# Two gate projections tied behind the layer's last conv transposes, and these transposes spread over four PSUM banks

## Chip, cores and metric

The kernel runs on one NeuronCore of a Trainium2 chip. The metric is the device time of one execution in microseconds; the time before is the median of three runs, 2527.41 us.

## What is computed

A trunk of two layers on 512 tokens of width 1024, all in float32. Each layer applies a half-step SwiGLU FFN, gated parallel token mixers, and a second half-step FFN. The change is in the mixer, where three branches A, B and C are computed from one input projection, gated and summed; B is the convolution module:

```
h = _rmsnorm(x, mix_norm_pre[l])
proj = h @ w_in[l]
...
ob = _conformer_conv(conv_in, conv_w[l], conv_b[l], conv_norm_g[l], conv_norm_b[l])
...
gates = jax.nn.sigmoid(gate_pre + b_gate[l]).reshape(b, s, N_BRANCH, D_MODEL)
merged = gates[:, :, 0] * ya + gates[:, :, 1] * yb + gates[:, :, 2] * yc
x = x + _rmsnorm(merged @ w_out[l], mix_norm_post[l])
```

`_conformer_conv` is a GLU, a causal depthwise convolution of width 31 over 512 channels, a LayerNorm over the channels, and a silu; `yb` is its result times `w_proj_b`, and `gates[:, :, 1]` is the sigmoid of 1024 columns of `proj`.

## The kernel before

A float32 product runs as three matmuls: each operand is split into a rounded part (`hi`, ScalarE, line 120) and the rest (`lo`, VectorE, line 121), and lines 138, 139 and 140 multiply lo by hi, hi by hi and hi by lo. Weights come by the sync queue in pieces of 1 MB (`raw`, two buffers) and are split into `hi` and `lo` tiles, four of each. A gate projection (`gate`, through `proj_t`) is eight such triples, 24 matmuls of 512 columns, into a bank of tag `pm`; ScalarE then takes the sigmoid into `gt` (line 751).

PSUM has eight banks, by tag: three `pm`, two `ps`, two `pt`, one `po`. `ps` and `pt` serve the attention before this place and the FFNs.

The order of the instructions on each engine is set by a scheduler from the order of the program text and from what each instruction waits for. `tc.issue_after(x)` adds an edge: what is issued within comes behind `x` on its engine. The convolution is done on VectorE as 31 multiply-adds for each of four chunks of 128 channels (`taps`, line 498, tiles `y`, list `ys`). They are queued, and each split releases some of them behind itself. What is left when branches A and C are done is tied behind the last multiply of a gate (`flush`, line 758).

Then, for the convolution branch, in this order of the text:

- lines 778 to 789: for each of four groups of 128 tokens, four transposes (line 781, one per channel chunk) bring `ys` to tokens in one bank; VectorE takes statistics (lines 784, 785), ScalarE the square root (line 214, in `rstd`), VectorE the reciprocal (line 215) and the normalization into `yn` (line 788);
- lines 790 to 794: for each channel chunk, four transposes (line 793) bring `yn` back to channels in a `pt` bank, and ScalarE applies the silu (line 794);
- lines 795 to 797: the results are split into `ob` pairs (lines 464, 465);
- lines 798 to 809: for four pairs of output chunks, two gates and two products with `ob` (`branch`, lines 138 to 140, then line 758), the sum with the other branches on GpSimd (line 806), and the split of the sum (lines 808, 809).

ScalarE loads a table (ACT_TABLE_LOAD) when it goes from one of square root, sigmoid and silu to another.

Of the kernel before, what the change touches and what calls it, by code (L numbers as in the profile page):

```python
# [18 lines left out]
P = 128  # L19
# [30 lines left out]
def kernel(ctx: ExitStack, tc: tile.TileContext, a, out):  # L50
    nc = tc.nc
    V, S, G, PE, SY = nc.vector, nc.scalar, nc.gpsimd, nc.tensor, nc.sync

    def bc(t):
        return t.bitcast(F32)
# [7 lines left out]
    def bank(tag, shape=(P, T)):  # L63
        return psum.tile(list(shape), F32, tag=tag, name=tag, bufs=BANKS[tag])
# [24 lines left out]
    ident = per.tile([P, P], F32, name="ident")  # L89
# [24 lines left out]
    def split(raw, into=None):  # L114
        if into is None:
            hi = wp.tile(list(raw.shape), F32R, tag="hi", name="hi", bufs=HLB)
            lo = wp.tile(list(raw.shape), F32R, tag="lo", name="lo", bufs=HLB)
        else:
            hi, lo = into
        S.activation(hi, raw, AF.Copy)  # L120
        last = V.tensor_sub(lo, raw, bc(hi))  # L121
        for _ in range(min(pace[0], len(tapq))):
            tapq.pop(0)(last)
        return hi, lo
# [6 lines left out]
    def col_chunks(src, c0, c1, step=256):  # L131
        for c in range(c0, c1, step):
            raw = load(src[:, c:c + step], KD, step)
            for s in range(0, step, P):
                yield c + s, split(raw[:, :, s:s + P])
# [6 lines left out]
    def proj_group(chunks, hh, hl):  # L142
        ps = [bank("pm") for _ in chunks]
        for p_, (wh, wl) in zip(ps, chunks):
            for k in range(KD):
                mm3(p_, wh[:, k, :], wl[:, k, :], hh[:, k, :], hl[:, k, :], k == 0, k == KD - 1)
        return ps
# [63 lines left out]
    def rstd(ms, tag, bias=None, scale=1.0):  # L211
        n = ms.shape[1]
        r = sp.tile([P, n], F32, tag="rstd" + tag, name="rstd", bufs=4 if n == 1 else 1)
        S.activation(r, ms, AF.Sqrt, bias=eps[:, 0:1] if bias is None else bias, scale=scale)
        V.reciprocal(r, r)
        return r
# [217 lines left out]
    def mixer(l):  # L434
# [5 lines left out]
        def proj_t(chunk):  # L440
            return proj_group([chunk], hh, hl)[0]

        mrg = tc.tile_pool(name="mrg", bufs=1, side="right", reuse_waits="tile")
        with tc.tile_pool(name="mix", bufs=1, reuse_waits="tile") as mp:
# [13 lines left out]
            def ztile(n, name):  # L458
                return mp.tile([P, n], F32, tag="zr", name=name, bufs=ZRB)
# [12 lines left out]
            with tc.tile_pool(name="att", bufs=1, reuse_waits="tile") as ap:  # L472
                ys = []
# [189 lines left out]
                for h in range(4):  # L663
                    for i in range(NT):
                        V.tensor_scalar_mul(oc[h][:, i, :], oc[h][:, i, :], orr[:, h * 4 + i:h * 4 + i + 1])
                    pt = bank("pt")
# [9 lines left out]
                for b in range(NT):  # L676
# [3 lines left out]
                    for h in range(4):  # L680
                        r = slice(64 * (h % 2), 64 * (h % 2) + 64)
                        ps = bank("ps", (P, n))
# [12 lines left out]
                for r4 in range(4):  # L695
                    po = bank("po", (P, 4, HD))
                    cols = slice(r4 * P, (r4 + 1) * P)
                    for h in range(4):
                        r = slice(64 * (h % 2), 64 * (h % 2) + 64)
                        ps = bank("ps", (P, 256))  # L700
# [26 lines left out]
                for f in range(2):  # L727
                    pt = bank("pt", (P, 4, P))
# [9 lines left out]
            def mpair(d):  # L738
                return tuple(gp.tile([P, T], F32R, tag=f"m{u}{d}", name="m" + u) for u in "hl")

            gch = [col_chunks(wi, GT0 + b * D, GT0 + (b + 1) * D) for b in range(3)]

            def gate(b, d, first):
                ps = proj_t(next(gch[b])[1])
                gt = ztile(T, "gt")
                bias = late[:, b * 8 + d:b * 8 + d + 1]
                if first:
                    S.activation(gt, ps, AF.Copy)
                    S.activation(gt, gt, AF.Sigmoid, bias=bias)
                else:  # L750
                    S.activation(gt, ps, AF.Sigmoid, bias=bias)
                return gt

            def branch(gt, wh, wl, k0, hls):
                ps = bank("pm")
                for k, (mh, ml) in enumerate(hls):
                    mm3(ps, wh[:, k0 + k, :], wl[:, k0 + k, :], mh, ml, k == 0, k == len(hls) - 1)
                return V.tensor_mul(gt, gt, ps)

            for dp in range(0, KD, 2):  # L760
                gts = [[gate(b, dp + j, dp == 0) for j in range(2)] for b in (2, 0)]
                wca = wp.tile([P, KD, 256], F32, tag="raw", name="wca", bufs=2)
                cols = slice(dp * P, (dp + 2) * P)
                SY.dma_start(wca[:, 0:4, :], a["w_proj_c"][l][:, cols].rearrange("(k p) n -> p k n", p=P))
                SY.dma_start(wca[:, 4:6, :], a["w_proj_a"][l][:, cols].rearrange("(k p) n -> p k n", p=P))
                for j in range(2):
                    wh, wl = split(wca[:, 0:6, j * P:(j + 1) * P])
                    branch(gts[0][j], wh, wl, 0, oc_hl)
                    flush = branch(gts[1][j], wh, wl, 4, oa_hl)
                    m_ = ring(F32, "m")  # L770
                    G.tensor_add(m_, gts[0][j], gts[1][j])
                    ms.append(m_)
# [3 lines left out]
            pace[0] = 0  # L776
            yn = []
            for t in range(NT):
                pn = bank("pt")
                for c in range(NCH):  # L780
                    PE.transpose(pn[:, c * P:(c + 1) * P], ys[c][:, t * P:(t + 1) * P], ident)
                bs = sp.tile([P, 6], F32, tag="bs", name="bs")
                mv = sp.tile([P, 2], F32, tag="mv", name="mv", bufs=4)
                V.bn_stats(bs, pn)
                V.bn_aggr(mv, bs)
                r = rstd(mv[:, 1:2], "ln")
                n_ = sp.tile([P, T], F32, tag="t2k", name="yn", bufs=5)
                V.tensor_scalar(n_, pn, mv[:, 0:1], r, op0=ALU.subtract, op1=ALU.mult)
                yn.append(n_)
            for c in range(NCH):  # L790
                pt = bank("pt")
                for t in range(NT):
                    PE.transpose(pt[:, t * P:(t + 1) * P], yn[t][:, c * P:(c + 1) * P], ident)
                S.activation(ys[c], pt, AF.Silu, bias=cbn[:, c:c + 1], scale=cg[:, c:c + 1])
# [1 line left out]
            for c in range(NCH):  # L796
                put(ob_hl[c], ys[c])
            for dp in range(0, KD, 2):
                gts = [gate(1, dp + j, False) for j in range(2)]
                wb = wp.tile([P, KD, 256], F32, tag="raw", name="wb", bufs=2)  # L800
                cols = slice(dp * P, (dp + 2) * P)
                SY.dma_start(wb[:, 0:4, :], a["w_proj_b"][l][:, cols].rearrange("(k p) n -> p k n", p=P))
                for j in range(2):
                    wh, wl = split(wb[:, 0:4, j * P:(j + 1) * P])
                    branch(gts[j], wh, wl, 0, ob_hl)
                    G.tensor_add(gts[j], gts[j], ms[dp + j])
                    mm.append(mpair(dp + j))
                    S.activation(mm[dp + j][0], gts[j], AF.Copy)
                    V.tensor_sub(mm[dp + j][1], gts[j], bc(mm[dp + j][0]))
# [27 lines left out]
    for l in range(L):  # L837
        ffn(a["ffn1_norm_pre"][l], a["ffn1_norm_post"][l], a["ffn1_w_gate"][l], a["ffn1_w_up"][l], a["ffn1_w_down"][l],
            (gain0[0], raws0) if l == 0 else None)
        mixer(l)  # L840
        ffn(a["ffn2_norm_pre"][l], a["ffn2_norm_post"][l], a["ffn2_w_gate"][l], a["ffn2_w_up"][l], a["ffn2_w_down"][l])
# [62 lines left out]
```

## Time and profile before

| | us |
|---|---|
| median of three runs | 2527.41 (2525.86 to 2529.16) |
| the profiled execution | 2526.2 |
| its span | 2524.4 |
| TensorE busy in the span | 2465.5 |
| VectorE busy | 1735.6 |
| ScalarE busy | 1174.8 |
| GpSimd busy | 246.9 |

The span goes from the first to the last instruction of the profiled execution; its own time is 1.8 us longer. Times in views are counted from the start of the span. PE is TensorE's matmuls, PEld its weight loads (which overlap the matmuls), DVE is VectorE, ACT ScalarE, SPq the issue of a transfer by the sync engine. A matmul is listed with its start and the time to its modelled end; the next starts before that end, so the pace is read from the starts. A row of the timeline ends with the idle time ahead of it on its engine and what ended it, in brackets, where there was some.

### The profile page before, as it was taken

How to read it: one execution, taken by the hardware profiler on the slowest of the kernel's cores; microseconds unless marked ns; L12 is line 12 of the kernel's file. 1: busy time of each engine (PE TensorE's matmuls, PEld its weight loads, DVE VectorE, ACT ScalarE, POOL GpSimd, SP SyncE). 2: the span in 40 equal slices, each digit the busy share in tenths (PEclk: the TensorE clock that was granted, in tenths of full speed). 3: DMA queues.
4: the chain of work that ended last, by engine and by line, in shares of the span. 5: the costliest groups of instructions: out<-in, count | busy, mean ns of one | idle time of the engine just before them, and what ended most of it. 6: DMA issues, size and time to landing. Idle time of an engine off the chain costs nothing.

```text
span 2524.4 us, 36883 instructions
## 1 busy us (share of the span) xinstructions
PE 2465.5 (98%) x14956; PEld 2190.3 (87%) x14956; DVE 1735.6 (69%) x2354; ACT 1174.8 (47%) x1953; POOL 246.9 (10%) x156
## 2 busy tenths in 40 slices
PE   8999999999999999999989999999899999999999
PEld 8999888778787889998889998887787878899987
DVE  8777554796577487775497774546965764877753
ACT  5545444633523354445454454446235244544552
POOL 0000012060011110000000000130600111100000
PEclk9999999999999999999999999999999999999999
DMA  4333335242132423333233332451421224233322
GB/s 160 105 108 114 105 123 169 73 129 81 43 96 76 162 72 108 110 101 109 76 106 112 101 108 101 136 163 54 133 89 39 92 75 159 76 101 101 110 100 75
DMA packets 211850, 261.92 MB, mean 104 GB/s; under 512 B 8160, under 2 KB 167264, under 8 KB 211424
## 3 DMA queue, kind: packets, MB, share of 16 engines
q1 hardware_dynamic: 204000, 249.06, 30.1%
q10 hardware_dynamic: 7680, 10.50, 1.6%
q8 instruction: 118, 1.93, 0.3%
q14 instruction: 52, 0.43, 0.1%
HBM read 237.47 MB, written 6.29 MB: 97 GB/s over the span
## 4 chain that ended last, share of the span: by engine, by line
PE 88%; DVE 7%; ACT 2%; issue 2%; DMA 1%; SPq 0%; DVEq 0%; ACTq 0%
PE pm L138 11%; PE pm L139 11%; PE pm L140 11%; PE ps L308 6%; PE ps L314 6%; PE ps L313 6%; PE pm L313 2%; PE pm L308 2%; PE pm L314 2%; DVE y L498 2%; PE ps L139 2%; PE ps L140 2%; PE ps L138 2%; DVE lo L121 2%; PE pt L140 2%; PE pt L138 2%
## 5 line engine op out<-in xcount | busy, mean ns | idle before, releaser
L121 DVE TENSOR_TENSOR lo<-raw,hi 128x1024 fp32r<-128x1024 f32 x354 | 458.5, 1296 | 380.3 <-ACT hi L120 380.3
L120 ACT ACTIVATE hi<-raw 128x1024 fp32r<-128x1024 f32 x354 | 373.7, 1057 | 324.0 <-PE ps L139 127.2
L138 PE MATMUL pm<-hb,lo 128*128 128x512 f32 (+1 forms) x848 | 325.0, 383 | 0.0
L139 PE MATMUL pm<-hb,hi 128*128 128x512 f32 (+1 forms) x848 | 324.2, 382 | 0.0
L140 PE MATMUL pm<-hb,hi 128*128 128x512 f32 (+1 forms) x848 | 323.7, 382 | 0.0
L308 PE MATMUL ps<-t,lo 128*128 128x256 f32 x960 | 272.2, 284 | 4.3 <-ACT pm L381 4.3
L314 PE MATMUL ps<-t,hi 128*128 128x256 f32 x960 | 271.7, 283 | 0.0
L313 PE MATMUL ps<-t,hi 128*128 128x256 f32 x960 | 271.6, 283 | 0.0
L121 DVE TENSOR_TENSOR lo<-s,hi 128x1024 fp32r<-128x1024 f32 x160 | 194.9, 1220 | 69.1 <-ACT hi L120 68.9
L498 DVE SCALAR_TENSOR_TENSOR y<-z,ppl,y 128x512 f32<-128x512 f32 x240 | 214.4, 894 | 4.1
L120 ACT ACTIVATE hi<-s 128x1024 fp32r<-128x1024 f32 x160 | 164.8, 1052 | 88.4 <-DVE s L379 87.2
L308 PEld LDWEIGHTS ps<-t,lo 128*128 128x128 f32 x960 | 184.2, 192 | 5.3 <-ACT pm L381 5.3
L138 PEld LDWEIGHTS pm<-hb,lo 128*128 128x128 f32 x848 | 159.6, 188 | 31.9 <-issue 1.8
L139 PEld LDWEIGHTS pm<-hb,hi 128*128 128x128 f32 x848 | 159.5, 188 | 29.9 <-issue 0.7
L140 PEld LDWEIGHTS pm<-hb,hi 128*128 128x128 f32 x848 | 159.5, 188 | 29.9 <-issue 0.8
L314 PEld LDWEIGHTS ps<-t,hi 128*128 128x128 f32 x960 | 184.3, 192 | 0.0
L313 PEld LDWEIGHTS ps<-t,hi 128*128 128x128 f32 x960 | 184.3, 192 | 0.0
L240 POOL TENSOR_TENSOR h<-x,gain 128x512 f32<-128x512 f32 x40 | 54.0, 1370 | 1128.8 <-DVE x L299 1087.8
L120 ACT ACTIVATE ih<-inner 128x512 fp32r<-128x512 f32 x176 | 106.0, 622 | 82.6 <-PE ps L140 49.1
L121 DVE TENSOR_TENSOR il<-inner,ih 128x512 fp32r<-128x512 f32 x176 | 118.0, 687 | 38.3 <-ACT ih L120 38.3
L308 PE MATMUL pm<-hb,lo 128*128 128x256 f32 x480 | 135.8, 283 | 0.0
L313 PE MATMUL pm<-hb,hi 128*128 128x256 f32 x480 | 135.8, 283 | 0.0
(331 smaller groups left out, 6153.9 us busy)
## 6 DMA issues: line engine op xcount, KB each, us to landing
raw<-in_w_in_dram SPq DMA_DIRECT2D x62, 1024.0 KB, 5.4
raw<-in_ffn_w_gate_dram SPq DMA_DIRECT2D x43, 1024.0 KB, 5.0
raw<-in_ffn_w_up_dram SPq DMA_DIRECT2D x43, 1024.0 KB, 5.0
raw<-in_ffn_w_down_dram SPq DMA_DIRECT2D x40, 1024.0 KB, 4.9
sw<-raw ACTq DMA_DIRECT2D x160, 64.0 KB, 2.0
raw<-in_w_out_dram SPq DMA_DIRECT2D x8, 1024.0 KB, 4.9
raw<-in_ffn_w_down_dram SPq DMA_DIRECT2D x8, 512.0 KB, 3.4
xd<-x SPq DMA_DIRECT2D x16, 256.0 KB, 3.6
```

What stands on the lines that cost most here:

```text
L120: S.activation(hi, raw, AF.Copy)
L121: last = V.tensor_sub(lo, raw, bc(hi))
L138: PE.matmul(ps, sl, mh, start=first, stop=False, skip_group_check=not check)
L139: PE.matmul(ps, sh, mh, start=False, stop=False, skip_group_check=not check)
L140: PE.matmul(ps, sh, ml, start=False, stop=last, skip_group_check=not check)
L240: G.tensor_mul(h[j], xs[t][:, j * T:(j + 1) * T], g[:, j * T:(j + 1) * T])
L308: PE.matmul(dst[:, f, :], sl, m[:, 0, :], start=start and f == 0 and k == 0, stop=False, skip_group_check=True)
L313: PE.matmul(dst[:, f, :], sh, m[:, 0, :], start=False, stop=False, skip_group_check=True)
L314: PE.matmul(dst[:, f, :], sh, m[:, 1, :], start=False, stop=k == 3, skip_group_check=True)
L498: V.scalar_tensor_tensor(y, z[:, j:j + T], cw[:, c, j:j + 1], y, op0=ALU.mult, op1=ALU.add)
```

## The change

`gate` gets a fourth argument. With it, the projection's matmuls come behind the given instruction on TensorE. The transposes of `ys` alternate between the tags `pt` and `ps`, so the four token groups have four banks. The first two gates of branch B are issued in the text ahead of the transposes back (`lead`), behind the last transpose of `ys` (`turn`), and no longer at the head of the loop over `dp`.

```
-            def gate(b, d, first):
-                ps = proj_t(next(gch[b])[1])
+            def gate(b, d, first, after=None):
+                chunk = next(gch[b])[1]
+                if after is None:
+                    ps = proj_t(chunk)
+                else:
+                    with tc.issue_after(after.ins):
+                        ps = proj_t(chunk)
...
             for t in range(NT):
-                pn = bank("pt")
+                pn = bank(("pt", "ps")[t % 2])
                 for c in range(NCH):
-                    PE.transpose(pn[:, c * P:(c + 1) * P], ys[c][:, t * P:(t + 1) * P], ident)
+                    turn = PE.transpose(pn[:, c * P:(c + 1) * P], ys[c][:, t * P:(t + 1) * P], ident)
...
+            lead = [gate(1, j, False, turn) for j in range(2)]
             for c in range(NCH):
...
-                gts = [gate(1, dp + j, False) for j in range(2)]
+                gts = lead if dp == 0 else [gate(1, dp + j, False) for j in range(2)]
```

In the changed kernel line 781 has become 786, 784 and 785 are 789 and 790, 788 is 793, 793 is 799, 794 is 800, 751 is 756, 758 is 763, 808 is 814.

The order of the instructions moves at three places of each layer. On TensorE, the first two groups of the transposes of `ys` in the kernel before (tile `y`; `hb` is the normalized input, so `pm<-hb` is a gate's matmul):

```order
L140 MATMUL pm<-oa,hi 128x512
L781 MATMUL pt<-ident,y 128x128 x6
L138 MATMUL pm<-hb,lo 128x512
```

```order
L140 MATMUL pm<-hb,hi 128x512
L781 MATMUL pt<-ident,y 128x128 x2
L138 MATMUL pm<-hb,lo 128x512
L139 MATMUL pm<-hb,hi 128x512
L140 MATMUL pm<-hb,hi 128x512
```

Thirty gate matmuls stand between these two pieces before, and eighteen more between the second and the last eight transposes of `ys`. The same place now, from the last matmul of branch A on:

```order
L140 MATMUL pm<-oa,hi 128x512
L786 MATMUL pt<-ident,y 128x128 x3
L786 MATMUL ps<-ident,y 128x128 x3
L786 MATMUL pt<-ident,y 128x128 x3
L786 MATMUL ps<-ident,y 128x128 x3
L786 MATMUL pt<-ident,y 128x128
L786 MATMUL ps<-ident,y 128x128
L786 MATMUL pt<-ident,y 128x128
L786 MATMUL ps<-ident,y 128x128
L138 MATMUL pm<-hb,lo 128x512
L139 MATMUL pm<-hb,hi 128x512
L140 MATMUL pm<-hb,hi 128x512
```

All sixteen stand ahead of the 48 gate matmuls, the four of the last channel chunk at their end; the sixteen transposes back (line 799) follow the 48.

On ScalarE, from the splits of the first `w_proj_b` weights to the silu, before:

```order
L120 ACTIVATE hi<-wb 128x512 x2
L751 ACTIVATE gt<-pm,late 128x512
L120 ACTIVATE hi<-raw 128x1024
L214 ACT_TABLE_LOAD
L214 ACTIVATE rstd<-mv,eps 128x1 x2
L751 ACT_TABLE_LOAD
L751 ACTIVATE gt<-pm,late 128x512
L120 ACTIVATE hi<-raw 128x1024
L214 ACT_TABLE_LOAD
L214 ACTIVATE rstd<-mv,eps 128x1 x2
L794 ACT_TABLE_LOAD
L794 ACTIVATE y<-pt,ppl 128x512 x2
```

and now:

```order
L120 ACTIVATE hi<-wb 128x512 x2
L214 ACT_TABLE_LOAD
L214 ACTIVATE rstd<-mv,eps 128x1 x4
L756 ACT_TABLE_LOAD
L756 ACTIVATE gt<-pm,late 128x512
L120 ACTIVATE hi<-raw 128x1024
L756 ACTIVATE gt<-pm,late 128x512
L800 ACT_TABLE_LOAD
L800 ACTIVATE y<-pt,ppl 128x512 x2
L464 ACTIVATE ob<-y 128x512
```

The four square roots stand together ahead of both sigmoids, and the second sigmoid directly ahead of the silu's table load.

On VectorE, from the last gate multiply of branches A and C on, now:

```order
L763 TENSOR_TENSOR gt<-gt,pm 128x512 x2
L498 SCALAR_TENSOR_TENSOR y<-z,ppl,y 128x512
L121 TENSOR_TENSOR lo<-wb,hi 128x512
L498 SCALAR_TENSOR_TENSOR y<-z,ppl,y 128x512 x7
L789 BN_STATS bs<-pt 128x6
L789 BN_STATS bs<-ps 128x6
L790 BN_AGGR mv<-bs 128x2 x2
```

Down to the seven taps these rows are those of the kernel before; behind them the weight split that stood among the first statistics has moved behind the normalizations.

## Rows read from the trace of the kernel before

**Rows 1.** The page, first part: busy time, share of the span, instructions.

```profile
PE 2465.5 (98%) x14956; PEld 2190.3 (87%) x14956; DVE 1735.6 (69%) x2354; ACT 1174.8 (47%) x1953; POOL 246.9 (10%) x156
```

**Rows 2.** Waits view, TensorE, whole run: us in total, times, longest.

```profile
PE pt L793 <- DVE rstd L215: 7.0, 2, 3.5
...
PE pt L781 <- DVE y L498: 2.1, 2, 1.0
```

**Rows 3.** Timeline, TensorE, 789.8 to 830: start, duration, instruction, idle ahead.

```profile
790.36 0.82 PE L781 MATMUL pt<-ident,y 128*128 128x128 f32 x6
799.05 0.44 PE L781 MATMUL pt<-ident,y 128*128 128x128 f32 x2 [1.03 <-DVE y L498]
803.43 1.15 PE L781 MATMUL pt<-ident,y 128*128 128x128 f32 x8
808.07 3.89 PE L793 MATMUL pt<-ident,yn 128*128 128x128 f32 x16 [3.48 <-DVE rstd L215]
```

**Rows 4.** Timeline, VectorE, the last taps.

```profile
790.55 0.69 DVE L758 TENSOR_TENSOR gt<-gt,pm 128x512 f32<-128x512 f32 x1 [0.68 <-PE pm L140]
...
791.82 1.79 DVE L121 TENSOR_TENSOR lo<-wb,hi 128x512 fp32r<-128x512 f32 x1
793.53 5.46 DVE L498 SCALAR_TENSOR_TENSOR y<-z,ppl,y 128x512 f32<-128x512 f32 x7
```

**Rows 5.** Stretches: length, busy time of each engine (x), granted clock, DMA share, GB/s.

```profile
790.36:799.05 8.69, 7.67 (x37) 6.10 (x35) 8.23 (x10) 2.90 (x4) 1.74 (x1) 1.00 0.18 62
...
808.07:811.71 3.64, 3.62 (x16) 2.68 (x17) 0.89 (x2) 2.52 (x5) 0.00 (x0) 0.53 0.83 276
811.71:816.00 4.29, 4.29 (x22) 3.57 (x21) 2.47 (x4) 2.75 (x5) 0.00 (x0) 1.00 0.00 0
...
562.60:572.70 10.10, 5.57 (x24) 5.28 (x25) 10.06 (x8) 0.00 (x0) 6.48 (x4) 0.50 0.33 117
```

**Rows 6.** Timeline, TensorE: first matmul of a gate, and the 25th from it.

```profile
833.57 0.39 PE L138 MATMUL pm<-hb,lo 128*128 128x512 f32 x1
...
839.01 0.39 PE L138 MATMUL pm<-hb,lo 128*128 128x512 f32 x1
```

**Rows 7.** Timeline, VectorE: the last normalization.

```profile
808.03 0.81 DVE L788 TENSOR_SCALAR yn<-pt,mv,rstd 128x512 f32<-128x512 f32 x1
```

**Rows 8.** Timeline: a gate's last matmul and sigmoid; silu table load, first two silus.

```profile
771.09 0.39 PE L140 MATMUL pm<-hb,hi 128*128 128x512 f32 x1
...
771.51 0.69 ACT L751 ACTIVATE gt<-pm,late 128x512 f32<-128x512 f32 x1 [3.96 <-PE pm L140]
...
807.08 1.28 ACT L794 ACT_TABLE_LOAD   x1
...
809.41 1.63 ACT L794 ACTIVATE y<-pt,ppl 128x512 f32<-128x512 f32 x2 [1.05 <-PE pt L793]
```

**Rows 9.** Timeline, TensorE, behind the wait that ends at 564.90.

```profile
564.90 0.58 PE L138 MATMUL pm<-hi,hb 128*128 128x256 f32 x1 [5.23 <-DVE qk L526]
565.29 0.41 PE L139 MATMUL pm<-hi,hb 128*128 128x256 f32 x1
...
566.99 0.41 PE L138 MATMUL pm<-hi,hb 128*128 128x256 f32 x1
569.63 0.58 PE L138 MATMUL pm<-hi,hb 128*128 128x256 f32 x1 [2.23 <-DVE qk L526]
...
573.07 0.28 PE L138 MATMUL pm<-hi,hb 128*128 128x256 f32 x1
...
574.14 0.28 PE L138 MATMUL pm<-hi,hb 128*128 128x256 f32 x1
```

**Rows 10.** Page, sixth part (KB each, us to landing); timeline, that load and its first use.

```profile
raw<-in_w_in_dram SPq DMA_DIRECT2D x62, 1024.0 KB, 5.4
...
806.72 0.37 SPq L128 DMA_DIRECT2D raw<-in_w_in_dram  x1
...
823.48 1.05 ACT L120 ACTIVATE hi<-raw 128x1024 fp32r<-128x1024 f32 x1
```

## Prediction

> **What bounds the kernel now.** The page's first part comes first: TensorE is busy for 98% of the span, the next engine for 69% [rows 1]. So a change pays or costs only where it changes what TensorE does in the remaining 2%, or how fast its clock runs. The waits view of TensorE over the whole run then tells where the convolution branch stands in those 2%: it waits 2.1 us in all for the last taps and 7.0 us for the LayerNorm, twice each, once per layer [rows 2]. The two layers agree to 0.1 us, so I work out layer 0 and double it.
>
> TensorE's timeline of that place shows four steps [rows 3]. Six transposes of `ys` run at 790.36. Gate matmuls follow until the last tap's column is due. Two transposes run at 799.05, after a wait of 1.03 us for VectorE. More gate matmuls follow, then eight transposes at 803.43, a wait of 3.48 us, and the sixteen transposes back from tokens at 808.07. VectorE's timeline says what the 799.05 hangs on: the multiply at 790.55, then eight taps and a split, the last seven taps from 793.53 to 798.99 [rows 4]. The stretches view gives what the 3.48 us cost beside themselves: TensorE's granted clock is 1.00 up to the wait and 0.53 of full over the 3.64 us behind it, which is about 3.4 us at 1.2 GHz; from 811.71 on it is 1.00 again [rows 5].
>
> So the 48 matmuls of the first two gates already fill TensorE, most of them under the taps, the others under the first half of the LayerNorm. The question is which of the two waits is the longer without them.
>
> **The change, step by step** (layer 0, the path on TensorE from 790.36 to the first `ob` matmul, 811.71 in the kernel before).
>
> *Four banks.* All sixteen transposes of `ys` now stand together: twelve that need only the first three channel chunks, then four that need the last tap, then the gates. The number of transposes is the same. Sixteen take some 2.3 us at 0.14 us each (six in 0.82, eight in 1.15 [rows 3]) before and after: cost nothing.
>
> *The wait for the taps.* Nothing in VectorE's rows ahead of the statistics moves, and no tap can start before the multiply at 790.55, so the last tap still ends at 798.99 and its transpose still starts at 799.05 [rows 3, 4]. TensorE has only twelve transposes to do before it: 790.36 + 12 x 0.137 = 792.0. It then waits 799.05 - 792.0 = 7.0 us in place of 1.0: **+6.0 us**. Queued behind the waiting transpose is all of TensorE's work, and after it everything. The tie puts the gates there; they were what covered this wait.
>
> *The LayerNorm wait.* After 799.05 TensorE now has four transposes (0.6 us) and all 48 gate matmuls. Twenty-four take 839.01 - 833.57 = 5.44 us [rows 6], so 48 take 10.9 us and end at 810.5 or later. The kernel before has its last normalized tile at 808.03 + 0.81 = 808.84 [rows 7], with two gate activations and two table loads of ScalarE in between; now ScalarE takes all four square roots in a row. Even at the old pace it is done before 810.5. The 3.48 us go: **-3.5 us**. The work that hides it is the gates, with 1.7 us to spare.
>
> *The transposes back.* They now start when the second gate's matmuls end; call that S. ScalarE must first take that gate's sigmoid, which starts 0.42 us after the last matmul's start (771.09 to 771.51), or S + 0.2, and takes 0.69 us; only then comes the table load of 1.28 us for the silu [rows 8]. Before, that load was over at 808.36, ahead of the first silu. Now the first silu starts at S + 2.2, and the first two, which took 1.63 us together, end at S + 3.8. There are two `pt` banks: eight transposes fit at once, the next four wait for the first silu, the last four for the second. So the first `ob` matmul can start at S + 3.8 + 4 x 0.14, S + 4.4 us. Before, the same sixteen took 3.64 us, at the low clock [rows 5]: **+0.8 us**. The `ob` splits keep their places behind the silus; one weight split of ScalarE now stands among them, but matmuls of the next gate pair lie between the `ob` matmuls and cover it: nothing. The sync queue's next load waits for that split. It went out at 806.72 for a first use at 823.48 and needs 5.4 us to land [rows 10]; if it now goes out near S + 8.5, about 820, and its use moves to about 828, 8 us are left: nothing.
>
> *The clock.* Behind the 3.48 us wait some 3.4 us ran at 1.2 GHz. The other long wait, 5.23 us at 564.90, shows more: clock 0.50 for over ten microseconds, of which another wait takes 2.23 [rows 5, 9]. A wait of 7.0 us will do no less than the first. The pace at either level: eight matmuls of 256 columns take 566.99 - 565.29 = 1.70 us at the low clock (0.213 each), nine take 574.14 - 573.07 = 1.07 at the full one (0.119), a ratio of 1.79 [rows 9]. Work of 3.4 us at the low clock loses 3.4 x (1 - 1/1.79) = 1.5 us. As bounds I take 0, as behind the 1.03 us wait, and 2.5 us, from the 5.6 us of busy TensorE in the stretch of rows 9. I choose **+1.5 us**: as behind the 3.48 us wait, dense work follows the restart without a second wait. What the low clock cost before is already inside the 3.64 us.
>
> Sum: 6.0 - 3.5 + 0.8 + 1.5 = +4.8 us a layer, +9.6 us for two. The profiled execution took 2526.2 us, which gives 2535.8. The median of the three runs, 2527.41, lies 1.2 us above it, so I say **2536 us**, 0.4% slower. Nothing downstream takes it back: TensorE bounds there too.
>
> **Rivals.** 0.2% of this kernel, 5.1 us, is about what a measurement can tell from no change.
>
> *The gates pass the waiting transposes.* If TensorE did the gates' matmuls while the four transposes wait for the tap, the four banks would only shorten the LayerNorm. VectorE would have four statistics, two and two in 1.29 us, and four normalizations of 0.81 from 799.4 on, done near 806.2; with the 3.64 us behind it, 809.9 in place of 811.7: 1.8 us a layer, 2522.6 us, not slower. It decides if the wait at the taps stays below some 2.2 us (7.0 less 4.8). Against it: at 799.05 gate matmuls with ready operands stood behind the waiting transpose and TensorE idled 1.03 us, and the order of the changed kernel has all 48 behind it. Chance 0.04.
>
> *A second fall of the clock.* In the transposes back TensorE now waits some 1.8 us and does little for 4.4; the clock fell before over a wait of 3.48 us [rows 3, 5]. If it falls again over the `ob` matmuls, another 1.5 us a layer: 2526.2 + 12.6 = 2538.8 us. For the clock, transposes count as work by the rows: between 808.07 and 811.71 TensorE did nothing else, and from 811.71 on the row has 1.00 [rows 5]. The Trainium skill's page "TensorE: Matmul & The Clock Gate", Part 4 on the PE-mode transpose, has it otherwise: there the transpose mode does not engage the full clock, as it does not count as busy in the same way. By that rule this fall is the likely case; the trace disagrees with it here, at 16 transposes in 3.64 us, but not for thinner ones. Chance 0.17.
>
> *The clock stays full.* Then the terms are 3.3 us a layer: 2532.8 us, still slower. The drop behind the shorter wait speaks against it. Chance 0.10.
>
> **How the numbers follow.** The forecast has 0.62; the remaining 0.07 is what I have not seen, a silu table that loads sooner or a longer low clock among it. The range takes the full-clock case at its low end, 2532, and at the high end both the 2.5 us bound and the second fall, 2 x 7.3 = 14.6 us: 2541. Slower by over 0.2%: the forecast, both clock rivals and a little of the rest, 0.90; within 0.2%: the passing gates and the rest, 0.07; faster 0.03.
>
> **What would show it.** Right: one wait of TensorE near 7 us at line 786 for the taps, none for the LayerNorm; a stretch at half clock over the first gate's matmuls; a wait near 1.8 us for ScalarE within line 799; the first `ob` matmul 4 to 6 us later than 811.7. The tap term is wrong if the last tap ends much before 799, the transposes' term if the silu table is loaded before the second gate ends, the clock term if that stretch shows 1.00. The whole is wrong if TensorE runs gate matmuls between 792 and 799.

## The result, and the profile after

The changed kernel took 2542.21 us (median of five runs, 2539.77 to 2548.86) against 2528.16 us for the kernel before (five runs too): a ratio of 1.0057, 95% interval 1.0043 to 1.0070, 14 us slower. Run once more beside the variants below, on one chip with seventeen runs of the kernel before, it took 2540.28 us against 2530.01: 1.0038 (1.0026 to 1.0051), 10 us slower. The forecast had the direction and its four terms, each within 0.4 us a layer; the first of the two times lies 1 us above its range, the second within it.

The waits view of TensorE, over the whole run of the changed kernel, answers to [rows 2]: us in total, times, longest.

```profile
PE pt L786 <- DVE y L498: 14.4, 2, 7.2
...
PE pt L799 <- ACT y L800: 4.0, 2, 2.0
```

The wait for the taps went from 1.03 to 7.2 us in each layer, the wait for the LayerNorm is no longer in the list, and a wait of 2.0 us in each layer for the silu is new. The timeline of TensorE in layer 0 answers to [rows 3]; the profiled execution is 4.5 us late when it comes here, so lengths are to be compared, not times.

```profile
794.88 0.49 PE L786 MATMUL pt<-ident,y 128*128 128x128 f32 x3
...
803.54 0.47 PE L786 MATMUL pt<-ident,y 128*128 128x128 f32 x1 [7.19 <-DVE y L498]
...
816.79 1.03 PE L799 MATMUL pt<-ident,yn 128*128 128x128 f32 x8
819.82 1.33 PE L799 MATMUL pt<-ident,yn 128*128 128x128 f32 x8 [2.00 <-ACT y L800]
```

VectorE's timeline shows why the first wait is so long: the multiply behind which the taps are tied, and the last seven taps, stand as far apart as in [rows 4] (2.94 us from start to start, 2.98 before). The third row is the last normalization of the LayerNorm.

```profile
795.08 0.69 DVE L763 TENSOR_TENSOR gt<-gt,pm 128x512 f32<-128x512 f32 x1 [0.68 <-PE pm L140]
...
798.02 5.46 DVE L498 SCALAR_TENSOR_TENSOR y<-z,ppl,y 128x512 f32<-128x512 f32 x7
...
809.50 0.80 DVE L793 TENSOR_SCALAR yn<-ps,mv,rstd 128x512 f32<-128x512 f32 x1
```

ScalarE's timeline around the transposes back: the second gate's sigmoid, the table load behind it, and only then the first two silus, 2.2 us after the first transpose back.

```profile
816.99 0.69 ACT L756 ACTIVATE gt<-pm,late 128x512 f32<-128x512 f32 x1 [2.47 <-PE pm L140]
817.69 1.28 ACT L800 ACT_TABLE_LOAD   x1
818.99 1.45 ACT L800 ACTIVATE y<-pt,ppl 128x512 f32<-128x512 f32 x2
```

The stretches of this place, with the granted clock (the column after the five engines), answer to [rows 5].

```profile
794.88:803.54 8.66, 1.47 (x13) 1.23 (x12) 8.19 (x10) 1.92 (x2) 1.71 (x1) 0.83 0.19 61
803.54:807.40 3.86, 3.86 (x11) 3.23 (x12) 3.31 (x10) 0.94 (x4) 0.00 (x0) 0.50 0.00 0
807.40:816.79 9.39, 9.39 (x43) 7.67 (x42) 4.12 (x8) 2.94 (x4) 0.00 (x0) 1.00 0.00 1
816.79:821.01 4.22, 2.21 (x18) 1.64 (x16) 0.02 (x1) 3.99 (x6) 0.00 (x0) 1.00 0.00 0
821.01:824.40 3.39, 3.39 (x10) 2.71 (x9) 1.97 (x3) 3.39 (x6) 0.00 (x0) 0.52 0.00 0
```

There are two falls of the clock in place of one: over the first gate's matmuls, behind the wait for the taps, and a second one over the `ob` matmuls, behind the transposes back. Layer 1 shows the same two. The two profiled executions lie 22.7 us apart, more than the medians: the one of the changed kernel is the slowest of its five runs. The place of the change and the falls at it make 12.8 us of that; the rest lies elsewhere, where its profile has falls of the clock (near 384, 933, 1288 and 2200 us) that the profile before has not, against one the other way; such falls come and go (last section).

### The profile page after: what moved, and what is told of

It reads as the page before. It is cut to its first block, busy times and chain, and to the rows that moved or that the text cites. A ratio compares the mean times of both kernels' runs of the same rounds, so it can differ in the third digit from the quotient of the medians.

```text
span 2547.1 us, 36885 instructions
## 1 busy us (share of the span) xinstructions
PE 2477.1 (97%) x14956; PEld 2201.5 (86%) x14956; DVE 1737.5 (68%) x2354; ACT 1172.1 (46%) x1951; POOL 247.9 (10%) x156
## 4 chain that ended last, share of the span: by engine, by line
PE 88%; DVE 7%; ACT 2%; issue 2%; DMA 2%; SPq 0%; DVEq 0%; ACTq 0%
PE pm L138 11%; PE pm L139 11%; PE pm L140 11%; PE ps L308 6%; PE ps L314 6%; PE ps L313 6%; PE pm L314 2%; PE pm L313 2%; PE pm L308 2%; PE ps L139 2%; PE ps L140 2%; PE ps L138 2%; DVE y L498 2%; PE pt L140 2%; PE pt L138 2%; PE pt L139 2%
```

## Experiments

"The place" is the path on TensorE from the first transpose of `ys` to the first `ob` matmul; it took 21.35 us before and 26.13 us after, 21.4 and 26.2 in layer 1. Two theories stood against each other at the start. The one is that the tie takes the cover from the taps, that the thin work lets the clock fall twice, and that the banks cost nothing. The other is that the banks, through the order that the scheduler then gives to ScalarE, are the cost.

**Four banks alone.** The kernel before with one line changed:

```
-                pn = bank("pt")
+                pn = bank(("pt", "ps")[t % 2])
```

> The kernel before with four banks for the transposes of ys and nothing else; its gates stay where the scheduler puts them (27 of their matmuls ahead of the last four transposes, 21 behind). 'The place' is the path on TensorE from the first transpose of ys to the first ob matmul: 21.4 us in the kernel before, 26.1 us in the changed one. Theory (the tie costs, the banks do not): the taps are covered again, the wait for them is near 1 us, the LayerNorm takes all four groups at once, and a wait of some 2 us is left before the transposes back; place 18.5 to 20.5 us, clock 1.00 throughout, 2 us a layer less than before, 2522 to 2527 us in all. Rival (the banks cost, by another order of the square roots and sigmoids on ScalarE): place 22 us or more, 2530 us or more.

It took 2532.42 us (eleven runs) against 2530.55, ratio 1.0010 (1.0001 to 1.0019). Its place is 20.97 us, above what the theory gave and below the kernel before. TensorE's timeline, ScalarE's, and the stretches:

```profile
797.95 0.33 PE L781 MATMUL pt<-ident,y 128*128 128x128 f32 x1 [1.05 <-DVE y L498]
...
803.82 0.33 PE L793 MATMUL pt<-ident,yn 128*128 128x128 f32 x1 [0.31 <-DVE yn L788]
804.74 1.16 PE L793 MATMUL pt<-ident,yn 128*128 128x128 f32 x6 [0.59 <-DVE yn L788]
808.60 1.97 PE L793 MATMUL pt<-ident,yn 128*128 128x128 f32 x8 [2.71 <-ACT y L794]
```

```profile
804.82 0.69 ACT L751 ACTIVATE gt<-pm,late 128x512 f32<-128x512 f32 x1
805.41 1.05 ACT L120 ACTIVATE hi<-raw 128x1024 fp32r<-128x1024 f32 x1
806.47 1.28 ACT L794 ACT_TABLE_LOAD   x1
807.77 1.45 ACT L794 ACTIVATE y<-pt,ppl 128x512 f32<-128x512 f32 x2
```

```profile
789.25:803.24 13.99, 12.94 (x66) 10.59 (x64) 13.16 (x23) 4.35 (x8) 1.74 (x1) 1.00 0.11 38
803.24:810.22 6.98, 3.31 (x17) 2.38 (x16) 3.84 (x7) 6.90 (x10) 0.00 (x0) 0.79 0.17 34
810.22:814.10 3.88, 3.88 (x11) 3.12 (x10) 2.13 (x4) 2.64 (x5) 0.00 (x0) 0.50 0.59 209
```

The taps are covered (1.05 us), and of the LayerNorm's wait 0.31 and 0.59 us are left. But the transposes back take 7.0 us, since the second sigmoid, a weight split and the table load stand ahead of the first silu, and the clock falls over the `ob` matmuls, where I had expected 1.00 throughout: from the first of them to the thirtieth matmul it is 8.5 us (8.8 in layer 1) and 6.7 before. What the four banks give is lost there, and the total missed the 2522 to 2527 us of the theory. The rival was half right, in kind, with some 2 us where the change costs 10 to 14.

**The tie with two banks.** The changed kernel with `bank("pt")` in that line.

> The changed kernel with two banks for the transposes of ys, the tie kept. Theory: TensorE waits near 8 us for the taps with six transposes done, then again some 3 us for the first normalization to free a bank, and only then come the gates; place 29 to 33 us, two falls of the clock, 2550 us or more. Rival (the number of banks does not matter once the tie is there): place near 26 us, 2540 to 2544 us.

It took 2550.42 us (four runs), ratio 1.0081 (1.0067 to 1.0094); the place is 30.0 us in both layers. TensorE waits three times:

```profile
799.14 0.69 PE L786 MATMUL pt<-ident,y 128*128 128x128 f32 x2 [7.84 <-DVE y L498]
802.55 2.01 PE L786 MATMUL pt<-ident,y 128*128 128x128 f32 x8 [2.72 <-DVE rstd L215]
819.06 1.79 PE L799 MATMUL pt<-ident,yn 128*128 128x128 f32 x8 [2.00 <-ACT y L800]
```

So the banks save the change 3.9 us a layer of the tie's own cost; the tie without them is worse, as the theory had it.

**The wait for the taps filled.** The changed kernel with 28 matmuls of 512 columns between the twelfth and thirteenth transposes of `ys`, into a bank that nobody reads; the last four transposes follow in a loop of their own:

```
+            fill = bank("po")
+            for _ in range(28):
+                with tc.issue_after(turn.ins):
+                    turn = PE.matmul(fill, hb[:, 0, 0, 0:P], hb[:, 0, 0, :], start=True, stop=True, skip_group_check=True)
```

> The changed kernel with 28 matmuls of 512 columns, whose result nobody reads, between the twelfth and the thirteenth transpose of ys: some 6.4 us of work within the 7 us wait for the taps. Theory (the idle TensorE lets its clock fall, and that costs some 1.8 us of the place): the wait shrinks below 1 us, the gates run at 0.23 us from the first on, the place falls from 26.1 to 24.0 to 24.6 us; the second fall, behind the transposes back, stays; 2537 to 2540 us. Rival (the place is long by the wait alone): place 26 us, 2542 us.

It took 2536.83 us (six runs), ratio 1.0024 (1.0013 to 1.0035). The place is 24.33 us in both layers, against 26.13. Work that does nothing makes the changed kernel faster there; by the total alone, 6 us over the kernel before, it could not be told from the second measurement of the changed kernel, whose interval overlaps. The stretches:

```profile
794.48:803.18 8.70, 7.87 (x42) 6.39 (x40) 8.23 (x10) 1.92 (x2) 1.74 (x1) 1.00 0.18 60
803.18:814.59 11.41, 11.41 (x52) 9.46 (x53) 7.43 (x17) 3.88 (x7) 0.00 (x0) 1.00 0.00 1
...
818.81:822.20 3.39, 3.39 (x17) 2.80 (x16) 1.97 (x3) 3.39 (x6) 0.00 (x0) 1.00 0.02 5
...
2078.74:2082.10 3.36, 3.36 (x11) 2.67 (x10) 1.95 (x3) 3.36 (x6) 0.00 (x0) 0.55 0.00 0
```

Four transposes and 48 gate matmuls take 11.41 us at 1.00 (second row) where the changed kernel took 13.25: the first fall costs 1.8 us in that execution. The last two rows are the `ob` matmuls of the two layers. The second fall, which I expected in both, came in layer 1 alone, behind the same 4.2 us of transposes back.

**The wait for the silu filled.** The changed kernel with eight such matmuls between the eighth and ninth transposes back; each transpose back is tied behind the one before it, so that the eight keep their place.

> The changed kernel with 8 such matmuls between the eighth and the ninth transpose back, some 1.8 us of work within the 2 us wait for the silu. Theory (the thin stretch of transposes back lets the clock fall a second time, over the ob matmuls): place unchanged within 0.3 us, no fall at the ob matmuls, which run at 0.23 us from the first on, so 1.5 us a layer less: 2537 to 2541 us. Rival (the second fall comes from the transposes themselves, or from elsewhere): the clock still falls there, and the time stays at 2542 us or rises.

It took 2538.30 us (four runs), ratio 1.0037 (1.0023 to 1.0051). The stretches of the transposes back and the `ob` matmuls, layer 0 and layer 1:

```profile
814.28:818.50 4.22, 4.05 (x26) 3.03 (x24) 0.03 (x1) 3.99 (x6) 0.00 (x0) 1.00 0.00 0
818.50:822.00 3.50, 3.50 (x17) 2.91 (x16) 2.08 (x3) 3.50 (x6) 0.00 (x0) 1.00 0.00 0
...
2083.54:2087.00 3.46, 3.46 (x17) 2.87 (x16) 2.04 (x3) 3.46 (x6) 0.00 (x0) 1.00 0.00 0
```

The stretch of 4.22 us has its length still, and the clock does not fall in either layer. The place is 25.82 us in layer 0; in layer 1 it is 26.97, where the first fall lasted longer. So the second fall comes of that thin stretch, the wait and the transposes together, and the first stays without it. Here too the trace shows it and not the total, whose interval overlaps that of the second measurement.

**The changed kernel again, and one gate tied.** The second is the changed kernel with `gate(1, j, False, (None, turn)[j])`: the first gate is free.

> The changed kernel once more, beside the variants, on one chip. Theory (wait for the taps, transposes back, first and second fall of the clock, 6.0 - 3.5 + 0.8 + 1.8 + 1.6 us = 6.4 to 6.7 us a layer): 12 to 14 us over the kernel before; place 25.5 to 27.5 us in both layers, and low clock behind the transposes back in at least one.

> The changed kernel with the first gate free and only the second tied behind the last transpose. Theory (what costs is that nothing is left for the taps): the first gate's 24 matmuls, 5.4 us, fill the wait for the taps but for some 1.6 us; the second gate's 5.4 us cover most of the LayerNorm; no fall at the taps; the transposes back still wait for the second sigmoid and the silu's table; place 20 to 22 us, 4 to 6 us a layer less than with both tied; 2528 to 2534 us. Rival (any tie costs the place about as much): 25 us or more.

The changed kernel is told of above: 10.3 us over the kernel before, less than the 12 to 14 that I expected; its places are 25.80 and 25.92 us, as expected, with both falls in both layers. The stretches from the last tap's transpose to the first transpose back, and over the `ob` matmuls, in layer 0:

```profile
798.79:811.71 12.92, 12.92 (x53) 10.72 (x53) 7.43 (x17) 3.88 (x7) 0.00 (x0) 0.87 0.00 1
...
815.93:819.33 3.40, 3.40 (x10) 2.70 (x9) 1.98 (x3) 3.40 (x6) 0.00 (x0) 0.53 0.00 0
```

With one gate tied it is 2531.69 us (ten runs), ratio 1.0005 (0.9996 to 1.0014). The first gate covers most of the taps; TensorE's timeline:

```profile
804.39 0.33 PE L786 MATMUL pt<-ident,y 128*128 128x128 f32 x1 [1.73 <-DVE y L498]
...
815.05 1.97 PE L799 MATMUL pt<-ident,yn 128*128 128x128 f32 x8 [2.71 <-ACT y L800]
```

The wait for the taps is 1.7 us where 1.6 was worked out, with the clock at 1.00, and the place is 20.97 us, as with four banks alone; the clock falls over the `ob` matmuls here too. The tie itself is not the cost; what it takes away from the taps is.

**A late sigmoid, and a third gate.** Both have four banks and no tie. The second gate's sigmoid is tied behind the last silu, and the first two products with `ob` go to the `ps` banks; the second kernel computes three gate projections ahead of the transposes back, the first two:

```
+            pre = [proj_t(next(gch[1])[1]) for j in range(3)]
+            lead = [squash(1, 0, pre[0])]
...
+            with tc.issue_after(silu.ins):
+                lead += [squash(1, j, pre[j]) for j in range(1, len(pre))]
```

(`squash` is the sigmoid of `gate`; the other kernel has `range(2)`.)

> Four banks, no tie; the second gate's sigmoid stands behind the last silu on ScalarE instead of ahead of the first, and the first two products with ob go to the ps banks, so that the sigmoid may be late. Theory (the silu waits for the second sigmoid and for the table load behind it): with four banks alone the first silu started 4.5 us after the transposes back; here within 2 us; matmuls of the next gate pair, which the scheduler puts between the transposes back, cover what is left; no fall of the clock there; 2 to 4 us a layer less than with four banks alone, 2524 to 2528 us. Rival (the silu is late for the normalizations, not for the sigmoid): no shorter than four banks alone, 2531 us or more.

> As the late sigmoid, and a third gate's projection stands ahead of the transposes back: 27 gate matmuls at the taps, 45 over the LayerNorm. Theory (the place is bound by TensorE waiting, and there are enough matmuls whose operands are ready): no wait over 1.1 us, clock 1.00 throughout, 4 to 5 us a layer less than the kernel before, 2518 to 2523 us. Rival (the third gate's weight split on VectorE delays the LayerNorm by its 1.2 us and the waits come back further on): 2526 us or more.

The late sigmoid took 2517.20 us (six runs), ratio 0.9952 (0.9938 to 0.9965), the third gate 2516.17 us (six runs), 0.9941 (0.9928 to 0.9953), against 2530.01: 13 and 14 us faster than the kernel before, more than I gave them. The stretches of the late sigmoid (transposes back and `ob`), then of the third gate (from the taps on):

```profile
809.79:816.07 6.28, 6.28 (x37) 5.21 (x36) 4.00 (x7) 4.96 (x8) 0.00 (x0) 1.00 0.25 65
816.07:820.00 3.93, 3.93 (x20) 3.27 (x19) 0.69 (x1) 3.90 (x6) 0.00 (x0) 1.00 0.48 169
```

```profile
791.04:799.74 8.70, 7.63 (x41) 6.20 (x39) 8.22 (x10) 2.27 (x4) 1.74 (x1) 1.00 0.00 0
799.74:810.49 10.75, 10.75 (x49) 8.89 (x50) 7.88 (x18) 2.98 (x6) 0.00 (x0) 1.00 0.29 83
810.49:814.91 4.42, 4.41 (x27) 3.50 (x26) 0.92 (x2) 4.14 (x6) 0.00 (x0) 1.00 0.44 157
```

TensorE is busy throughout but for about 1 us at the taps, and the clock is at 1.00. With the late sigmoid the first silu still starts 3.1 us after the transposes back, not within 2; twenty matmuls of the next gate pair lie among them and hide it. Those matmuls are work that stands behind the place in the kernel before. At 0.227 us each [rows 6] they are 4.5 us of its 20.26; the 15.7 that are left are 5.6 us less than 21.35, which makes 11 of the 13 us in two layers. The third gate's place, 23.87 us, holds 34 such matmuls more than the kernel before, 7.7 us; by the same working it gives 10 of its 14 us. These are estimates, and the late sigmoid and the other banks for the products were not run apart, so how much each gives is not shown.

## Why the prediction was wrong, step by step

*The wait for the taps*, +6.0 us: it measured 7.19 against 1.03, +6.2. Right, and for the reason given: the last tap did not move.

*The LayerNorm wait*, -3.5 us: right; VectorE's last normalization ends at 810.30, 6.5 us before the transposes back start at 816.79.

*The transposes back*, +0.8 us: 4.22 against 3.64, +0.6, with the wait on the silu near the 1.8 us worked out (2.0) and its cause as given. Right.

*The clock behind the taps*, +1.5 us: 1.8 us, from the filled wait; set against the same 11.41 us, the second profile gives 1.5 and 1.6 (12.92 us, and 13.03 in layer 1). Right in kind and close in size. By themselves these four terms give +5.1. The sixteen transposes of `ys` and the 48 gate matmuls, whose order was put at no cost, take 12.9 us at the full clock (1.47 and 11.41) where they took 13.2 (21.35 less 1.03, 3.48 and 3.64). So the place measured +4.8. That this is the very sum of the forecast is in part luck: misses of 0.2 to 0.3 us cancel.

*The step that failed is the rival "a second fall of the clock"*, which had 0.17 and was left out of the sum. The clock fell over the `ob` matmuls in both layers of both profiled executions of the changed kernel. From the first `ob` matmul to the start of the thirtieth matmul it is 8.3 us there and 6.7 before: +1.6 a layer, where the rival gave 1.5. With it the sum is 6.4 us a layer, 12.8 in all; the two measurements, 14 and 10, lie on either side. In the second profile, of 2540.28 us, places and falls make 12.0 of the 14.1 us that it is longer than the profile before. I had judged from [rows 5] that transposes count as work for the clock, since it rose over nothing but sixteen transposes. That reading carried too far. Those sixteen stood in 3.64 us and brought the clock back; the same sixteen, begun at the full clock and with a wait of 2.0 to 2.7 us among them, did not hold it in eleven of the twelve layers profiled with such a wait: both layers of four banks alone, of one gate tied, of two banks tied and of the two executions of the changed kernel; in the filled taps one fell and one did not. The Trainium skill's page "TensorE: Matmul & The Clock Gate", Part 4, by which transposes do not count as busy in the same way, forecast this fall. On that rule the trace agrees at this fall, and not at the rise over sixteen transposes [rows 5]. Eight matmuls put among the transposes took the fall away in both layers. They filled the wait as well, so the runs do not tell whether the transposes count for nothing, for less, or in full, with the wait alone bringing the fall.

The range ended at 2541 because it set both falls, the first of them at its bound of 2.5 us, against the profiled execution of 2526.2 us: 14.6 us over the five-run median of 2528.16 would have been 2542.8. The forecast leans the same way: 2535.8 and the 1.2 us by which the median lay higher make 2537.0, not 2536. Over 2528.16 the 12.8 us of the account give 2541.0; the 1.2 us that are left lie within the interval.

## What to carry to other kernels

Before work is tied behind a wait, look at what covers that wait now: here the same matmuls had two waits to cover, and were moved from the longer to the shorter. Where TensorE is the bound, price its thin stretches for the clock as well as for their length, and if the price is in doubt give both cases weight. A better cure than choosing which wait to cover was to bring more ready work there, and to keep other tables' work on ScalarE from standing ahead of the result that TensorE waits for.

## What the runs showed that I had not expected

The clock's falls differ between executions of one kernel. Near the start of layer 1 the changed kernel waits 0.84 us and then 1.50 us, in both of its profiled executions. TensorE's timeline and the stretch behind the second wait, in the first execution, then in the second:

```profile
1277.80 0.38 PE L164 MATMUL pm<-hb,lo 128*128 128x256 f32 x1 [0.84 <-ACT hb L254]
...
1280.05 0.39 PE L171 MATMUL pm<-hb,hi 128*128 128x256 f32 x1 [1.50 <-DVE hb L255]
```

```profile
1280.05:1284.64 4.59, 4.59 (x38) 4.59 (x39) 4.28 (x10) 1.21 (x4) 1.41 (x2) 1.00 0.92 299
```

```profile
1273.31 0.38 PE L164 MATMUL pm<-hb,lo 128*128 128x256 f32 x1 [0.84 <-ACT hb L254]
...
1275.55 0.39 PE L171 MATMUL pm<-hb,hi 128*128 128x256 f32 x1 [1.50 <-DVE hb L255]
```

```profile
1275.55:1280.14 4.59, 4.59 (x25) 4.59 (x26) 4.17 (x9) 0.47 (x2) 1.41 (x2) 0.63 0.82 269
```

The same two waits carry a fall in the one (0.63, with 25 matmuls in 4.59 us) and none in the other (1.00, with 38). At the next FFN's start TensorE waits 2.3 us in every profile. The timeline and the stretch after the change, then before:

```profile
932.42 0.63 PE L252 MATMUL pt<-ident,h 128*128 128x128 f32 x4 [2.30 <-DVE h L249]
```

```profile
931.00:938.00 7.00, 5.58 (x35) 5.61 (x36) 7.00 (x9) 1.09 (x2) 0.00 (x0) 0.76 0.20 77
```

```profile
921.51 0.63 PE L252 MATMUL pt<-ident,h 128*128 128x128 f32 x4 [2.31 <-DVE h L249]
```

```profile
917.00:928.00 11.00, 8.69 (x74) 8.52 (x73) 11.00 (x14) 2.57 (x7) 2.89 (x2) 1.00 0.20 69
```

The clock fell here in six of the ten profiles: both of the changed kernel, two banks tied, one gate tied, the filled taps and the third gate. It did not in the kernel before, four banks alone, the filled silu wait and the late sigmoid. Whether the change has a part in this fall is not shown.

So a profile without a fall at a wait of this size does not show that the next execution has none. Single runs of one kernel spread over 0.35%, 2526.1 to 2534.9 us for the kernel before on one chip, more than the 0.2% that I had taken for what a measurement can tell from no change.
